# Dense experts: VectorE's instructions in the order of the source, and the source laid out for it

## The chip, the cores and the metric

The kernel runs on one core of one Trainium2 chip. The metric is the device time of one execution in microseconds; lower is better. Three runs of the kernel before gave 3190.89, 3192.01 and 3199.44 us; the median is 3192.01 us.

## The reference

One encoder block on 1024 tokens of width 1024: a mixer (differential attention and a short convolution, gated and summed), then a product-key expert layer (PEER), and a final norm. The change concerns the expert layer. For every token it is

```python
q = (xc @ w_query).reshape(c, 8, 2, 128)
sc = einsum('chpd,hpnd->chpn', q, sub_keys)            # 8 heads, 2 halves, 128 keys
# top 16 of each half, their 256 sums, top 16 of those: 16 of 16384 experts a head
eidx, g = chosen experts, softmax of their scores      # 128 experts a token
a = gelu(einsum('chkd,cd->chk', expert_u[eidx], xc))
out = einsum('chk,chkd->cd', g * a, expert_v[eidx])
```

with `expert_u` and `expert_v` of 16384 x 1024 values, float32. The result is added to h and normed.

## The kernel before

The 1024 tokens are 8 tiles of 128. The expert layer treats them in two ways at once.

*Dense.* For the first five tiles (`NB = 5`, 640 tokens) every expert is computed, 128 experts (one row of the key grid) at a time, in a loop of `NK = 128` rows. For row i `expert_in` (L916) loads u's 128 experts (`raw_rows`), splits them into a rounded high half and a low half (`split`, L893: ScalarE rounds to `uh`, VectorE subtracts to `uhl`), multiplies them with the tokens' two halves into PSUM (`z`: two column halves of 320, 24 matmuls each), applies Gelu on ScalarE (`pr`, L929), multiplies by the router weights `wt` on VectorE (L930; four rows of weights are one load from `w_d`), and splits the product (`ph` on ScalarE, `phl` on VectorE, by the same `split`). `expert_v` (L934) loads and splits the row's v (`vh`, `vhl`). Rows are taken in pairs (`BLK = 2`): `expert_out` (L946) adds a finished pair to the outputs during the two following rows, five of ten output groups in each, six matmuls of 512 columns a group. Four of the ten stay in PSUM (`held`); six go through a PSUM ring of two (`pout`) and are added to SBUF by VectorE (`hacc`, L957). So a row has 48 matmuls of 320 columns and 30 of 512, and on VectorE one `uhl`, `vhl`, `pr` and `phl` and three `hacc`.

*Gathered.* For the last three tiles (`NA = 3`) only the chosen experts are computed. `gather_gen` (L729) goes through 3 x 128 experts. For each, POOL issues an indirect DMA that brings every token's u and v (128 rows of 8 KB) into one of four slots (`uvt`, `UVT = 4`); VectorE takes the dot product with the token (L749), ScalarE applies Gelu and the softmax weight (`wt`, L751 and L752), and VectorE adds the scaled v to the accumulator (`acc`, L754), which also frees the slot. After 128 experts the tile is normed and stored (`last`, L762). The choice itself (`select_gen`, L594: top-16 searches, one-hot sums with a product on POOL, L639, and an exponential on ScalarE) runs for these tiles beside the dense rows, too.

What sets the order: the side jobs are Python generators. Every group of matmuls calls `tick` with its length in source microseconds (at 2.4 GHz, 12.8 us a row, 1638 for the loop), and a generator with a pace of p us makes one step for every p us ticked. The gather has two steps an expert (dot, accumulation) and a pace of `GATHER = 1.9`; a selection has 32 steps a tile, at 1.5 us for tile 5 and `SEL_STEP_D = 8` for tiles 6 and 7. That gives the order of the source. It is then the framework's scheduler that, by priority (order of the source) and readiness in a model of the machine's times, orders each engine's instructions, VectorE's too; on the chip every engine runs its list in that order. After the loop `finish_rows` adds, norms and stores the dense tiles, with the rest of the gather's steps between.

Of the kernel before, what the change touches and what calls it, by code (L numbers as in the profile page):

```python
# [10 lines left out]
F32 = mybir.dt.float32  # L11
# [4 lines left out]
AF = mybir.ActivationFunctionType  # L16
ALU = mybir.AluOpType
# [3 lines left out]
P = 128  # L21
S = 1024
D = 1024
NT = S // P
KD = D // P
NB = 5
NA = NT - NB
# [8 lines left out]
NK = 128  # L36
# [6 lines left out]
NE = PH * TOPK  # L43
# [4 lines left out]
BLK = 2  # L48
NR = 2
WB = 4  # L50
WT = 32
WQ = 4
WFB = 2
GATHER = 1.9
SEL_STEP = 1.5
SEL_STEP_D = 8
W_STEP = 1.6
MIXW = 3
ATT = (5, 4)
# [6 lines left out]
def block_kernel(ctx, tc, x, wqkv, wcols, wpr, wo, wq, skT, uv, uT, an_w, fn_w, fin_w, sub_w,  # L66
                 conv_w, lq1, lk1, lq2, lk2, cosT, sinT, out):
    nc = tc.nc
    V, A, PL, PE, SP = nc.vector, nc.scalar, nc.gpsimd, nc.tensor, nc.sync
# [72 lines left out]
    gens = []  # L142

    def start(gen, us):
        gens.append([gen, us, us])
        return gens[-1]
# [351 lines left out]
    def run(gen):  # L498
        for _ in gen:
            pass  # L500
# [158 lines left out]
    state, got = {}, {}  # L659

    def select_gen_all(t):
        for tt in range(NT):
            while tt not in ready:
                yield
            if tt < NB:
                ev = [state["wfe"].tile([P, NE], F32, name=f"e{j}", tag=f"e{j}", bufs=2) for j in range(3)]
                yield from select_gen(t, tt, ev[:2], ev[2])
                chosen.append(ev)
            else:
                yield from select_a(t, tt)  # L670
                yield SEL_STEP_D

    def select_a(t, tt):
        idx = idxp.tile([P, NE], I32, name="idx", tag="idx")
# [53 lines left out]
    def gather_gen(gat):  # L728
        st = {}  # L729

        def slot():
            return gat.tile([P, 2 * D], F32, name="uvt", tag="uvt", bufs=UVT)

        def fetch(c, k):
            if k == 0:
                st[c] = gat.tile([P, D], F32, name="hng", tag="hng")
                SP.dma_start(out=st[c], in_=hn_d[sels[c][0] * P:(sels[c][0] + 1) * P, :])
            t = slot()
            PL.indirect_dma_start(out=t[:], out_offset=None, in_=uv,  # L739
                                  in_offset=bass.IndirectOffsetOnAxis(ap=sels[c][1][:, k:k + 1], axis=0))  # L740
            return c, k, t

        def use(c, k, t):
            u, v = t[:, 0:D], t[:, D:2 * D]
            if k == 0:
                st["acc"] = gat.tile([P, D], F32, name="acc", tag="acc")
                SP.dma_start(out=st["acc"], in_=h_d[sels[c][0] * P:(sels[c][0] + 1) * P, :])
            zt = tiny.tile([P, 1], F32, name="zt", tag="zt")
            V.scalar_tensor_tensor(u, u, 1.0, st[c], op0=ALU.mult, op1=ALU.mult, accum_out=zt)  # L749
            wt = tiny.tile([P, 1], F32, name="wt", tag="wt")  # L750
            A.activation(wt, zt, AF.Gelu)  # L751
            A.activation(wt, wt, AF.Copy, scale=sels[c][2][:, k:k + 1])  # L752
            yield
            V.scalar_tensor_tensor(st["acc"], v, wt, st["acc"], op0=ALU.mult, op1=ALU.add)  # L754
            yield

        def fetch_last(c):
            t = slot()
            SP.dma_start(out=t[:, 0:D], in_=bass.AP(tensor=fin_w.tensor, offset=fin_w.offset, ap=[[0, P], [1, D]]))
            return t[:, 0:D], t[:, D:2 * D]  # L760

        def last(c, fw, junk):  # L762
            acc = st["acc"]
            ss = tiny.tile([P, 1], F32, name="ss_o", tag="ss_o")
            A.activation(junk, acc, AF.Square, accum_out=ss)
            r = rstd_of(ss, D, 1, "o")
            state["normed"] = c
            yield
            V.scalar_tensor_tensor(acc, acc, r, fw, op0=ALU.mult, op1=ALU.mult)
            SP.dma_start(out=out[sels[c][0] * P:(sels[c][0] + 1) * P, :], in_=acc)  # L770

        held = None
        for c in range(NA):
            while c >= len(sels):
                yield
            for k in range(NE):
                while k >= got[sels[c][0]]:
                    yield
                new = fetch(c, k)
                if held:  # L780
                    end = fetch_last(c - 1) if k == 0 else None
                    yield from use(*held)
                    if end:
                        yield from last(c - 1, *end)
                held = new
        end = fetch_last(NA - 1)
        yield from use(*held)
        yield from last(NA - 1, *end)

    selst, wfs, mts = ExitStack(), ExitStack(), ExitStack()  # L790
    for st in (selst, wfs, mts):
# [94 lines left out]
    ps_v = pspool("ps_v", 2, left)  # L886
    ps_r = pspool("ps_r", 1, left)
    du, dn, dv, hp, gat = (pool(n) for n in ("du", "dn", "dv", "hp", "gat"))
    gather = start(gather_gen(gat), GATHER)
    hacc = hp.tile([P, NB - NR, D], F32, name="hacc")  # L890
    held = [[ps_r.tile([P, 512], F32, name=f"held{t}{hf}") for hf in range(2)] for t in range(NR)]

    def split(t, tag, bufs, shape, eng):  # L893
        pl = du if tag == "uh" else dv
        hi = pl.tile(shape, F32R, name=tag, tag=tag, bufs=bufs)
        A.copy(out=hi, in_=t)  # L896
        lo = pl.tile(shape, F32R, name=f"{tag}l", tag=f"{tag}l", bufs=bufs)
# [13 lines left out]
    def raw_rows(src):  # L911
        t = du.tile([P, D], F32, name="raw", tag="raw", bufs=3)
        SP.dma_start(out=t, in_=src)
        return t

    def expert_in(i):  # L916
        b = i // WB
        if i % WB == 0:
            wts[b] = dn.tile([P, GB // WT, WB, WT], F32, name="wt", tag="wt", bufs=2)
            SP.dma_start(out=wts[b], in_=w_d[:, :, i:i + WB, :].rearrange("c p i t -> p c i t"))  # L920
        ur = raw_rows(uT[i])
        u = split(ur, "uh", 2, [P, D], V)
        us = [(u[0][:, k * P:(k + 1) * P], u[1][:, k * P:(k + 1) * P]) for k in range(KD)]
        hs = halves(GB)
        z = ps_z.tile([P, 2, 512], F32, name="z", tag="z")[:, :len(hs), :hs[0][1]]
        for j, (c0, cn) in enumerate(hs):
            passes(z[:, j, :], us, [(hh[:, k, c0:c0 + cn], hl[:, k, c0:c0 + cn]) for k in range(KD)], cn)
        p = dn.tile([P, GB], F32, name="pr", tag="pr", bufs=1)
        A.activation(p.rearrange("p (h c) -> p h c", h=len(hs)), z, AF.Gelu)  # L929
        V.tensor_mul(p.rearrange("p (c t) -> p c t", t=WT), p.rearrange("p (c t) -> p c t", t=WT),  # L930
                     wts[b][:, :, i % WB, :])
        return split(p, "ph", PHB, [P, GB], V)

    def expert_v(i):  # L934
# [8 lines left out]
            if q:  # L943
                order.append(q.pop(0))

    def expert_out(pv, vv, part, first, last):  # L946
        n = len(order) // BLK
        for t, hf in order[part * n:(part + 1) * n]:
            ds = slice(hf * 512, (hf + 1) * 512)
            lhs = [(p[0][:, t * P:(t + 1) * P], p[1][:, t * P:(t + 1) * P]) for p in pv]  # L950
            rhs = [(v[0][:, ds], v[1][:, ds]) for v in vv]
            if t < NR:
                passes(held[t][hf], lhs, rhs, 512, first, last)
            else:
                ps = ps_v.tile([P, 512], F32, name="pout", tag="v")
                passes(ps, lhs, rhs, 512)
                V.tensor_add(hacc[:, t - NR, ds], ps, hacc[:, t - NR, ds])  # L957
# [20 lines left out]
            SP.dma_start(out=out[t * P:(t + 1) * P, :], in_=ys[t])  # L978
            yield

    pv, vv = [], []
    for i in range(NK + BLK):
        if i < NK:
            pv.append(expert_in(i))
        b, part = i // BLK - 1, i % BLK
        if b >= 0:
            expert_out(pv[:BLK], vv[:BLK], part, b == 0, b == NK // BLK - 1)
            if part == BLK - 1:
                pv, vv = pv[BLK:], vv[BLK:]
        if i < NK:  # L990
            vv.append(expert_v(i))
        if i == 1:
            for t in range(NR, NB):
                SP.dma_start(out=hacc[:, t - NR, :], in_=h_d[t * P:(t + 1) * P, :])
# [9 lines left out]
        next(gather[0])  # L1004
    run(rows)
    run(gather[0])


def _pack(w, kt, cols):
# [50 lines left out]
```

## Time and profile before

| | |
|---|---|
| median of three runs | 3192.01 us |
| profiled execution, its own time | 3202.99 us |
| its span, first to last instruction | 3201.2 us |
| TensorE matmul busy | 3023.5 us, 94% |
| VectorE busy | 2648.8 us, 83% |
| ScalarE, POOL busy | 1300.8 us (41%), 928.5 us (29%) |
| DMA | 801 MB, mean 250 GB/s |

PE is TensorE's matmul, PEld its weight load, DVE VectorE, ACT ScalarE, POOL GpSimd, SP the engine that issues most DMAs. L905 is line 905 of the kernel; helpers (L905 for every dense matmul, L898 for every low half) have one line for all their uses, so groups go by tiles: `phl<-pr,ph` is the subtraction that writes `phl`. Times are microseconds from the start of the span, mean lengths nanoseconds. Matmuls overlap, and their ends are modelled: the pace of matmuls is read from a run of them, not from their lengths. A wait is put down to what was ready last. The dense loop lies between 1317 and 3158 us.

### The profile page before, as it was taken

How to read it: one execution, taken by the hardware profiler on the slowest of the kernel's cores; microseconds unless marked ns; L12 is line 12 of the kernel's file. 1: busy time of each engine (PE TensorE's matmuls, PEld its weight loads, DVE VectorE, ACT ScalarE, POOL GpSimd, SP SyncE). 2: the span in 40 equal slices, each digit the busy share in tenths (PEclk: the TensorE clock that was granted, in tenths of full speed). 3: DMA queues.
4: the chain of work that ended last, by engine and by line, in shares of the span. 5: the costliest groups of instructions: out<-in, count | busy, mean ns of one | idle time of the engine just before them, and what ended most of it. 6: DMA issues, size and time to landing. Idle time of an engine off the chain costs nothing.

```text
span 3201.2 us, 45898 instructions
## 1 busy us (share of the span) xinstructions
PE 3023.5 (94%) x17551; PEld 2773.3 (87%) x17551; DVE 2648.8 (83%) x4661; ACT 1300.8 (41%) x2341; POOL 928.5 (29%) x712
## 2 busy tenths in 40 slices
PE   7999999898989989799999999999999999999994
PEld 6799998798988879789989989899898999999993
DVE  5442466379999996799999999999988999999998
ACT  3322364336567766433333333333333333333332
POOL 2310000036344444222332322222222323332333
PEclk9999999999999989899999999999999999999997
DMA  4451232555444375769888888798888999998987
GB/s 179 145 181 66 83 113 79 199 172 212 145 171 168 135 282 190 255 246 329 311 282 328 316 292 307 278 329 314 302 318 319 345 342 335 341 347 321 340 318 276
DMA packets 237549, 801.11 MB, mean 250 GB/s; under 512 B 18832, under 2 KB 123280, under 8 KB 174096
## 3 DMA queue, kind: packets, MB, share of 16 engines
q0 software_dynamic: 64704, 442.53, 37.3%
q1 hardware_dynamic: 152592, 305.30, 27.6%
q10 hardware_dynamic: 20032, 50.34, 4.1%
q8 instruction: 138, 2.26, 0.3%
q14 instruction: 83, 0.68, 0.1%
HBM read 714.74 MB, written 83.36 MB: 249 GB/s over the span
## 4 chain that ended last, share of the span: by engine, by line
PE 40%; issue 21%; DVE 16%; POOL 9%; DMA 9%; ACT 4%; SPq 0%; POOLq 0%; ACTq 0%; DVEq 0%
PE z L905 9%; POOL uvt L739 8%; PE pout L905 5%; PE pg L228 4%; PE held L905 4%; PE pq L228 3%; DMA uvt<-in_uv,idx 3%; PE ph L228 3%; DVE acc L754 2%; PE py L228 2%; DVE uvt L749 2%; PE pw L695 1%; PE ps L376 1%; PE pv L228 1%; DVE ms L714 1%
## 5 line engine op out<-in xcount | busy, mean ns | idle before, releaser
L739 POOL DMA_INDIRECT uvt<-in_uv,idx x384 | 533.2, 1389 | 1288.1 <-DVE acc L754 937.3
L905 PE MATMUL z<-actTh,uhl 128*128 128x320 f32 x2048 | 638.0, 312 | 4.0 <-DVE uhl L898 4.0
L905 PE MATMUL z<-actTh,uh 128*128 128x320 f32 x2048 | 637.4, 311 | 4.0 <-ACT pr L929 3.0
L905 PE MATMUL z<-actTl,uh 128*128 128x320 f32 x2048 | 637.0, 311 | 0.0
L749 DVE SCALAR_TENSOR_TENSOR uvt<-uvt,hng 128x1024 f32<-128x1024 f32 x384 | 471.4, 1230 | 54.3 <-DMA uvt<-in_uv,idx 53.6
L754 DVE SCALAR_TENSOR_TENSOR acc<-uvt,wt,acc 128x1024 f32<-128x1024 f32 x384 | 495.0, 1289 | 1.6 <-ACT wt L752 1.2
L905 PEld LDWEIGHTS z<-actTh,uh 128*128 128x128 f32 x2048 | 387.7, 189 | 15.7 <-ACT pr L929 3.7
L905 PEld LDWEIGHTS z<-actTh,uhl 128*128 128x128 f32 x2048 | 388.3, 190 | 11.6 <-DVE uhl L898 5.6
L905 PEld LDWEIGHTS z<-actTl,uh 128*128 128x128 f32 x2048 | 387.8, 189 | 9.9
L905 PE MATMUL pout<-vh,ph 128*128 128x512 f32 x768 | 304.0, 396 | 26.9 <-DVE hacc L957 14.0
L905 PE MATMUL pout<-vhl,ph 128*128 128x512 f32 x768 | 302.6, 394 | 0.6 <-DVE vhl L898 0.6
L905 PE MATMUL pout<-vh,phl 128*128 128x512 f32 x768 | 301.8, 393 | 0.0
L957 DVE TENSOR_TENSOR hacc<-pout,hacc 128x512 f32<-128x512 f32 x384 | 260.1, 682 | 21.2 <-PE pout L905 20.5
L718 POOL TENSOR_TENSOR o<-ms,wtr 128x512 f32<-128x512 bf16 x160 | 203.5, 1314 | 254.8 <-PE pw L695 134.8
L185 DVE TENSOR_TENSOR wl<-wr,wh 128x2048 fp32r<-128x2048 f32 x66 | 157.8, 2392 | 113.0 <-ACT wh L184 112.8
L751 ACT ACTIVATE wt<-zt 128x1 f32<-128x1 f32 x384 | 77.0, 201 | 417.0 <-DVE uvt L749 410.8
L896 ACT CAST uh<-raw 128x1024 fp32r<-128x1024 f32 x128 | 134.3, 1049 | 211.3 <-DMA raw<-in_uT 204.5
L184 ACT CAST wh<-wr 128x2048 fp32r<-128x2048 f32 x74 | 141.1, 1908 | 168.0 <-DMA wr<-in_wq 44.7
L695 PE MATMUL pw<-o,o 128*128 128x128 f32 x1280 | 172.3, 288 | 36.9 <-POOL o L718 19.4
L695 PEld LDWEIGHTS pw<-o,o 128*128 128x128 f32 x1280 | 164.4, 202 | 44.7 <-POOL o L718 25.3
L929 ACT ACTIVATE pr<-z 128x640 f32<-128x640 f32 x128 | 90.1, 704 | 275.4 <-PE z L905 254.6
L905 PE MATMUL held<-vhl,ph 128*128 128x512 f32 x512 | 200.3, 392 | 0.1
(290 smaller groups left out, 6758.6 us busy)
## 6 DMA issues: line engine op xcount, KB each, us to landing
raw<-in_uT SPq DMA_DIRECT2D x128, 512.0 KB
raw<-in_uv SPq DMA_DIRECT2D x128, 512.0 KB
w_d<-wbuf ACTq DMA_DIRECT2D x20, 2048.0 KB
wt<-w_d SPq DMA_DIRECT2D x32, 1280.0 KB
wr<-in_wcols SPq DMA_DIRECT2D x28, 1024.0 KB
wr<-in_wq SPq DMA_DIRECT2D x24, 1024.0 KB
xt<-in_x SPq DMA_DIRECT2D x16, 512.0 KB
q_d<-qt POOLq DMA_DIRECT2D x32, 256.0 KB
```

The costliest lines, as they stand in the source:

```text
L184: A.copy(out=op[0][sl], in_=src)
L185: lo.tensor_sub(op[1][sl], src, op[0][sl].bitcast(F32))
L228: PE.matmul(pd, lhsT=l[a], rhs=r[b], start=i == 0 and j == 0, stop=i == n - 1 and j == len(c) - 1)
L695: PE.matmul(pw[:, u, :], lhsT=o2[:, t + u, :], rhs=o1[:, t + u, :], start=True, stop=True)
L718: PL.tensor_tensor(out=o1.rearrange("p t i -> p i t"), in0=ms[:, 0], in1=w[:, ts].unsqueeze(1).broadcast_to(sh), op=ALU.mult)
L739: PL.indirect_dma_start(out=t[:], out_offset=None, in_=uv, in_offset=bass.IndirectOffsetOnAxis(ap=sels[c][1][:, k:k + 1], axis=0))
L749: V.scalar_tensor_tensor(u, u, 1.0, st[c], op0=ALU.mult, op1=ALU.mult, accum_out=zt)
L754: V.scalar_tensor_tensor(st["acc"], v, wt, st["acc"], op0=ALU.mult, op1=ALU.add)
L896: A.copy(out=hi, in_=t)
L905: PE.matmul(ps, lhsT=lhs[k][a], rhs=rhs[k][b], start=first and k == 0 and j == 0, stop=last and k == n - 1 and j == 2)
L929: A.activation(p.rearrange("p (h c) -> p h c", h=len(hs)), z, AF.Gelu)
L957: V.tensor_add(hacc[:, t - NR, ds], ps, hacc[:, t - NR, ds])
```

## The change

In the dense stage, from just before the first row to the end of the kernel, VectorE's instructions are issued in the order of the source (`tc.manual_schedule`); the other engines are scheduled as before. The source is laid out anew:

- `expert_in` is taken apart. `expert_u(i+1)` (load and split of u) stands between the two halves of row i's z; `expert_z` ends with the Gelu; `expert_p` (product with the weights, split) stands behind the first of the row's five output groups.
- In the gather the dot of expert k stands ahead of the accumulation of k-1. A tile's h is loaded with its first gather. The normed tile is written to the second half of the slot that holds the norm's weights, no longer onto `acc`.
- The gather's pace is 2.36 us a step while the selection runs and 1.78 after it; a step of the selection comes every 13 us. The selection of tile 5 is brought to its first 64 experts before the loop.

```diff
-GATHER = 1.9
+GATHER = (2.36, 1.78)
-SEL_STEP_D = 8
+SEL_STEP_D = 13
...
             else:
                 yield from select_a(t, tt)
-                yield SEL_STEP_D
...
         def fetch(c, k):
             if k == 0:
...
+                st["acc", c] = gat.tile([P, D], F32, name="acc", tag="acc")
+                SP.dma_start(out=st["acc", c], in_=h_d[rows, :])
...
-        def use(c, k, t):
...
+        def dot(c, k, t):
+            u = t[:, 0:D]
             zt = tiny.tile([P, 1], F32, name="zt", tag="zt")
             V.scalar_tensor_tensor(u, u, 1.0, st[c], op0=ALU.mult, op1=ALU.mult, accum_out=zt)
             wt = tiny.tile([P, 1], F32, name="wt", tag="wt")
             A.activation(wt, zt, AF.Gelu)
             A.activation(wt, wt, AF.Copy, scale=sels[c][2][:, k:k + 1])
-            yield
-            V.scalar_tensor_tensor(st["acc"], v, wt, st["acc"], op0=ALU.mult, op1=ALU.add)
-            yield
+            return c, k, t, wt, fetch_last() if k == NE - 1 else None
...
+        def accumulate(c, k, t, wt, end):
+            acc = st["acc", c]
+            V.scalar_tensor_tensor(acc, t[:, D:2 * D], wt, acc, op0=ALU.mult, op1=ALU.add)
             yield
+            if end:
+                fw, y = end
+                ss = tiny.tile([P, 1], F32, name="ss_o", tag="ss_o")
+                A.activation(y, acc, AF.Square, accum_out=ss)
+                if c < NA - 1:
+                    yield
+                r = rstd_of(ss, D, 1, "o")
+                state["normed"] = c
+                yield
+                V.scalar_tensor_tensor(y, acc, r, fw, op0=ALU.mult, op1=ALU.mult)
+                SP.dma_start(out=out[sels[c][0] * P:(sels[c][0] + 1) * P, :], in_=y)
...
                 new = fetch(c, k)
                 if held:
+                    held = dot(*held)
+                    yield
+                    if dotted:
+                        yield from accumulate(*dotted)
+                    dotted = held
                 held = new
...
-    gather = start(gather_gen(gat), GATHER)
+    while not sels:
+        next(sel[0])
+    sel[1:] = [SEL_STEP_D, SEL_STEP_D]
+    ordered = ExitStack()
+    ordered.enter_context(tc.manual_schedule(engines={V.engine}))
+    gather = start(gather_gen(gat), GATHER[0])
...
+    def expert_u(i):
+        u = split(raw_rows(uT[i]), "uh", 2, [P, D], V)
+        return [(u[0][:, k * P:(k + 1) * P], u[1][:, k * P:(k + 1) * P]) for k in range(KD)]
+
+    def expert_z(i, us, mid):
...
         for j, (c0, cn) in enumerate(hs):
             passes(z[:, j, :], us, [(hh[:, k, c0:c0 + cn], hl[:, k, c0:c0 + cn]) for k in range(KD)], cn)
+            if j == 0:
+                mid()
         p = dn.tile([P, GB], F32, name="pr", tag="pr", bufs=1)
         A.activation(p.rearrange("p (h c) -> p h c", h=len(hs)), z, AF.Gelu)
+        return p
+
+    def expert_p(i, p):
         V.tensor_mul(p.rearrange("p (c t) -> p c t", t=WT), p.rearrange("p (c t) -> p c t", t=WT),
-                     wts[b][:, :, i % WB, :])
+                     wts[i // WB][:, :, i % WB, :])
         return split(p, "ph", PHB, [P, GB], V)
...
-    def expert_out(pv, vv, part, first, last):
+    def expert_out(pv, vv, part, first, last, after):
         n = len(order) // BLK
-        for t, hf in order[part * n:(part + 1) * n]:
+        for j, (t, hf) in enumerate(order[part * n:(part + 1) * n]):
+            if j == 1:
+                after()
...
-    pv, vv = [], []
+    pv, vv, us = [], [], [expert_u(0)]
     for i in range(NK + BLK):
+        b, part = i // BLK - 1, i % BLK
+        made = []
+        gather[2] = GATHER[sel not in gens]
+
+        def ahead():
+            if i + 1 < NK:
+                us.append(expert_u(i + 1))
+
+        def product():
+            if made:
+                pv.append(expert_p(i, made.pop()))
+
         if i < NK:
-            pv.append(expert_in(i))
...
+            made.append(expert_z(i, us.pop(0), ahead))
         if b >= 0:
-            expert_out(pv[:BLK], vv[:BLK], part, b == 0, b == NK // BLK - 1)
...
+            expert_out(pv[:BLK], vv[:BLK], part, b == 0, b == NK // BLK - 1, product)
+        product()
+        if b >= 0 and part == BLK - 1:
+            pv, vv = pv[BLK:], vv[BLK:]
         if i < NK:
             vv.append(expert_v(i))
```

## Rows read from the trace of the kernel before

**Rows 1.** The page's head: span; each engine's busy us, share, instructions.

```profile
span 3201.2 us, 45898 instructions
...
PE 3023.5 (94%) x17551; PEld 2773.3 (87%) x17551; DVE 2648.8 (83%) x4661; ACT 1300.8 (41%) x2341; POOL 928.5 (29%) x712
```

**Rows 2.** Busy time of each engine by stretch; the first line names the columns.

```profile
core 0: us, PE busy (x) PEld busy (x) DVE busy (x) ACT busy (x) POOL busy (x), PEclk, DMA share, GB/s
1346.00:1450.00 104.00, 98.85 (x531) 89.56 (x532) 100.11 (x207) 33.05 (x66) 27.44 (x18) 0.95 0.75 260
1450.00:2600.00 1150.00, 1135.90 (x6295) 1029.87 (x6295) 1091.74 (x1697) 392.51 (x801) 334.88 (x242) 1.00 0.87 313
2600.00:3147.00 547.00, 545.90 (x3040) 497.11 (x3039) 510.65 (x647) 189.41 (x403) 176.35 (x124) 1.00 0.91 334
3147.00:3201.20 54.20, 8.57 (x28) 5.24 (x26) 40.04 (x50) 12.26 (x34) 17.25 (x11) 0.61 0.69 247
sum 1855.20, PE 1789.22 PEld 1621.78 DVE 1742.55 ACT 627.23 POOL 555.92; mean PE 447.31 PEld 405.44 DVE 435.64 ACT 156.81 POOL 138.98
```

**Rows 3.** Pieces of the chain, 2100 to 2200 us: start us, us, what.

```profile
2144.42 4.10 PE held L905 x18
...
2151.57 5.04 PE z L905 x34
```

**Rows 4.** TensorE's waits from 1346 us on: us, times, longest.

```profile
PE pout L905 <- DVE hacc L957: 14.0, 10, 4.8
PE pout L905 <- ACT ph L896: 12.9, 1, 12.9
```

**Rows 5.** VectorE's waits from 1346 us on, same columns.

```profile
DVE uvt L749 <- DMA uvt<-in_uv,idx: 53.6, 48, 2.7
DVE hacc L957 <- PE pout L905: 20.5, 30, 1.9
DVE uhl L898 <- ACT uh L896: 15.1, 5, 7.6
DVE pr L930 <- ACT pr L929: 12.3, 14, 2.1
DVE pr L930 <- DMA wt<-w_d: 8.4, 1, 8.4
...
DVE phl L898 <- ACT ph L896: 0.2, 1, 0.2
```

**Rows 6.** Timeline of the end: start us, us, engine line op, what, count.

```profile
3157.77 0.40 PE L905 MATMUL pout<-vh,phl 128*128 128x512 f32 x1
...
3197.48 0.33 SPq L770 DMA_DIRECT2D out<-acc  x1
```

**Rows 7.** Timeline, VectorE and ScalarE at the first product.

```profile
1346.36 0.82 DVE L930 TENSOR_TENSOR pr<-pr,wt 128x640 f32<-128x640 f32 x1 [8.37 <-DMA wt<-w_d]
...
1347.10 0.08 DVE L590 MATCH_VALUE_LOAD tk<-sv,sc 128x8 f32 x1
...
1347.27 0.72 ACT L896 CAST ph<-pr 128x640 fp32r<-128x640 f32 x1 [11.14 <-DVE pr L930]
...
1348.09 0.80 DVE L898 TENSOR_TENSOR phl<-pr,ph 128x640 fp32r<-128x640 f32 x1
```

**Rows 8.** Timeline, a selection's product on POOL and phl beside it.

```profile
1409.76 2.85 POOL L639 TENSOR_TENSOR sc<-sc,sf 128x1024 bf16<-128x1024 bf16 x1 [0.48 <-DVE sc L637]
...
1410.73 2.57 DVE L898 TENSOR_TENSOR phl<-pr,ph 128x640 fp32r<-128x640 f32 x1
```

**Rows 9.** Pieces of the chain that are a gather, issue to use.

```profile
1421.49 11.22 DMA uvt<-in_uv,idx
...
1915.49 7.12 DMA uvt<-in_uv,idx
```

**Rows 10.** VectorE after 3147 us, groups: count, busy us, mean ns, idle.

```profile
L754 DVE SCALAR_TENSOR_TENSOR acc<-uvt,wt,acc 128x1024 f32<-128x1024 f32 x12 | 15.4, 1280 | 1.4 <-ACT wt L752 1.2
L749 DVE SCALAR_TENSOR_TENSOR uvt<-uvt,hng 128x1024 f32<-128x1024 f32 x10 | 12.2, 1220 | 7.1 <-DMA uvt<-in_uv,idx 7.0
```

More of the change, by code (lines that the diff above doesn't have):

```diff
@@ L736, in fetch @@
                 st[c] = gat.tile([P, D], F32, name="hng", tag="hng")
-                SP.dma_start(out=st[c], in_=hn_d[sels[c][0] * P:(sels[c][0] + 1) * P, :])
+                rows = slice(sels[c][0] * P, (sels[c][0] + 1) * P)
+                SP.dma_start(out=st[c], in_=hn_d[rows, :])
+                st["acc", c] = gat.tile([P, D], F32, name="acc", tag="acc")
+                SP.dma_start(out=st["acc", c], in_=h_d[rows, :])
             t = slot()
@@ L741, in fetch @@
             return c, k, t
-        def use(c, k, t):
[L744 to L747, printed above, removed]
+        def dot(c, k, t):
+            u = t[:, 0:D]
             zt = tiny.tile([P, 1], F32, name="zt", tag="zt")
@@ L752, in use, with fetch_last @@
             A.activation(wt, wt, AF.Copy, scale=sels[c][2][:, k:k + 1])
-            yield
-            V.scalar_tensor_tensor(st["acc"], v, wt, st["acc"], op0=ALU.mult, op1=ALU.add)
-            yield
-        def fetch_last(c):
+            return c, k, t, wt, fetch_last() if k == NE - 1 else None
+        def fetch_last():
             t = slot()
@@ L760, in fetch_last @@
             return t[:, 0:D], t[:, D:2 * D]
[L762 to L767, printed above, removed]
-            yield
-            V.scalar_tensor_tensor(acc, acc, r, fw, op0=ALU.mult, op1=ALU.mult)
-            SP.dma_start(out=out[sels[c][0] * P:(sels[c][0] + 1) * P, :], in_=acc)
-        held = None
+        def accumulate(c, k, t, wt, end):
+            acc = st["acc", c]
+            V.scalar_tensor_tensor(acc, t[:, D:2 * D], wt, acc, op0=ALU.mult, op1=ALU.add)
+            yield
+            if end:
[9 more added lines that the diff above has]
+                SP.dma_start(out=out[sels[c][0] * P:(sels[c][0] + 1) * P, :], in_=y)
+        held = dotted = None
         for c in range(NA):
@@ L780, in gather_gen @@
                 if held:
[L781 to L784, printed above, removed]
+                    held = dot(*held)
[3 more added lines that the diff above has]
+                    dotted = held
                 held = new
-        end = fetch_last(NA - 1)
-        yield from use(*held)
-        yield from last(NA - 1, *end)
+        held = dot(*held)
+        yield
+        yield from accumulate(*dotted)
+        yield from accumulate(*held)
     selst, wfs, mts = ExitStack(), ExitStack(), ExitStack()
@@ L914, in raw_rows @@
         return t
-    def expert_in(i):
+    def expert_u(i):
+        u = split(raw_rows(uT[i]), "uh", 2, [P, D], V)
+        return [(u[0][:, k * P:(k + 1) * P], u[1][:, k * P:(k + 1) * P]) for k in range(KD)]
+    def expert_z(i, us, mid):
         b = i // WB
@@ L920, in expert_in @@
             SP.dma_start(out=wts[b], in_=w_d[:, :, i:i + WB, :].rearrange("c p i t -> p c i t"))
-        ur = raw_rows(uT[i])
-        u = split(ur, "uh", 2, [P, D], V)
-        us = [(u[0][:, k * P:(k + 1) * P], u[1][:, k * P:(k + 1) * P]) for k in range(KD)]
         hs = halves(GB)
@@ L979, in finish_rows @@
             yield
-    pv, vv = [], []
+    pv, vv, us = [], [], [expert_u(0)]
     for i in range(NK + BLK):
+        b, part = i // BLK - 1, i % BLK
[7 more added lines that the diff above has]
+                pv.append(expert_p(i, made.pop()))
         if i < NK:
-            pv.append(expert_in(i))
-        b, part = i // BLK - 1, i % BLK
+            made.append(expert_z(i, us.pop(0), ahead))
         if b >= 0:
-            expert_out(pv[:BLK], vv[:BLK], part, b == 0, b == NK // BLK - 1)
-            if part == BLK - 1:
-                pv, vv = pv[BLK:], vv[BLK:]
+            expert_out(pv[:BLK], vv[:BLK], part, b == 0, b == NK // BLK - 1, product)
+        product()
+        if b >= 0 and part == BLK - 1:
+            pv, vv = pv[BLK:], vv[BLK:]
         if i < NK:
@@ L1006, in block_kernel @@
     run(gather[0])
+    ordered.close()
 def _pack(w, kt, cols):
```

## Prediction, before the changed kernel was run

> **What bounds the kernel now.** I read the page's head first. TensorE's matmuls are busy for 94% of the span and VectorE for 83%, ScalarE for 41% and POOL for 29% [rows 1]; so I asked how these two share the dense-expert stage. The table by stretches is the second view [rows 2]: from 1346 us, where the first router weights arrive, to 3147 us VectorE is busy for 100.1 + 1091.7 + 510.7 = 1702.5 of 1801 us, then for 40.0 of the last 54.2. The dense loop has 128 rows, so a row takes 1801/128 = 14.07 us.
>
> Is TensorE full in those rows? The third view is pieces of the chain in which it runs without a break [rows 3]: 5.04/34, so 0.148 us for a matmul of 320 columns, and 4.10/18, so 0.228 us for one of 512. A row has 2 x 24 of the first (z) and 5 x 6 of the second (five output groups, three passes for each row of the pair): 48 x 0.148 + 30 x 0.228 = 13.94 us. That is 0.13 us less than the measured row: TensorE is the bound, and its own waits in the stage are small (14.0 us on hacc, 12.9 us once at the start [rows 4]).
>
> VectorE is close behind. Its busy time from 1346 us on is 1742.5 us, 13.6 us a row. Its idle time is 1855.2 - 1742.5 = 112.7 us: 53.6 waiting for gathered experts, 20.5 for pout, 15.1 for uh, 12.3 + 8.4 for pr [rows 5], the rest at the end. The last stretch is the tail: TensorE's last matmul starts at 3157.77 us, and the last store is issued at 3197.48 us [rows 6]; in between VectorE ends the gathered experts that were left over.
>
> The Trainium skill (Perfetto Trace Analysis, "Identifying the Most-Contended Engine") says to judge TensorE's headroom not by matmul time but by the busy share of weight loads. That is 497.1/547 = 91% here and would leave 9%, some 160 us of the 1801; the cadence of rows 3 leaves 1%, and I go by the cadence.
>
> **The change part by part.** The arithmetic stays: the same dots, accumulations, subtractions and selections, so VectorE's 1742.5 us stay. What changes is the order, and in it what VectorE waits for.
>
> *Waits that go.* With VectorE late, pout is ready when hacc comes to it, and pr is made (the product stands behind the first output group): of 20.5 + 12.3 us I keep 5. The low half of u is made a row ahead, so of 15.1 us I keep 5, for late loads. Together 10 us (between 0 and 48).
>
> *A wait that comes: phl.* `expert_p` issues three things in a row: VectorE's product pr, ScalarE's rounding of it to ph, VectorE's subtraction phl. There is no step of a generator between them. Before, the scheduler put other work between product and subtraction, so phl waited only 0.2 us in all 128 rows. In the order of the source nothing can stand there. The price can be read at 1346 us [rows 7]: pr starts at 1346.36 and the next instruction on VectorE at 1347.10, so pr costs 0.74; ScalarE rounds from 1347.27 to 1347.99; phl starts at 1348.09, behind another instruction. Alone it could start between 1347.99 and 1348.09; I take 1348.03. VectorE would stand still from 1347.10 to there: 0.93 us. Times 128 rows: 119 us. From below 0.85 x 128 = 109, if the hand-overs are quicker; from above 135, since ScalarE is busy for 34% of the time [rows 2] and the rounding can come behind a cast: 34% of half of 0.72 us, 0.12 us a row more. Behind the waiting subtraction all of VectorE's queue stands: the gather's accumulations, and so POOL's next gathers, and hacc, and so TensorE's next output group. Nothing covers it: a row of VectorE's is 13.6 + 0.93 = 14.5 us, over TensorE's 13.94.
>
> *Selection in order.* Five half selections lie in the ordered stretch. Each waits twice for POOL's product (L639) and once for ScalarE's exponential. A POOL product lasts 2.85 us in the row shown, but in that same time phl takes 2.57 us [rows 8] where 0.80 is usual [rows 7]; so before, most of that time was lost as well. I take 10 x 1.1 + 5 x 1.0 = 16 us; bounds are 0 and 10 x 2.85 + 5 x 1.0 = 33. The Trainium skill (SBUF — State Buffer, "Who interferes with whom") has it that a VectorE instruction with two SBUF inputs and a GpSimd one that reads SBUF shut each other out; the two rows agree. By that rule the 11 us for POOL would be near 0, without it near 28.
>
> *The gather.* An expert's slot (there are four) is freed by its accumulation. Before, dot and accumulation alternate, and from the accumulation of expert k-4 to the dot of k there are 7 steps of 1.9 us of source pace; by the real row (14.07 for 12.8 us of pace) 14.6 us. Now the dot goes ahead, and there are 5 steps: 11.8 and 8.9 us of pace, and with rows of 14.9 us (12.8 of pace) 13.7 us in the first phase and 10.4 in the second. A gather takes 7.12 to 11.22 us from issue to use where it was waited for [rows 9]. So the first phase is covered and the second is at the edge. I take 30 us instead of 53.6: below 0, above 0.8 us (11.2 less 10.4) for each of some 168 experts of the second phase, 134 us. The phases: 80 steps of selection at 13 us make 1040 of 1638 us of pace, hence 1040/2.36 = 441 and 598/1.78 = 336 steps, 777 for 768 that are needed, so the gather ends with the loop.
>
> *The tail and the rest.* The tail's work is in the 1742.5 us already; its idle 14.2 us I keep (5 to 20). That the normalized rows go to another tile than acc frees acc before its store has landed; the next tile's acc now waits for its load twice. I set these against each other. The start is held by the weights at 1346 us as before.
>
> **Sum.** 1346 + 1742.5 + 119 + 16 + 30 + 10 + 14 = 3277.5 us of span. The profiled execution took 1.8 us more than its span and is 0.34% above the median, so 3279.3 x 0.9966 = 3268 us, 2.4% above 3192. All low ends together (1346 + 1742.5 + 109 + 5) give 3193 at the median, all high ends 3449. Neither is likely, and the ends aren't independent, since a longer row gives the gathers more time: its own range is 3210 to 3335.
>
> **Rivals.**
> *Faster, TensorE stays the bound.* TensorE could give back its 14.0 us on hacc, and if the gather ends with it, the experts that VectorE now does after 3147 us, 15.4 + 12.2 us [rows 10], leave the tail: 3201.2 - 14.0 - 27.6 = 3159.6 of span, 3150 at the median. VectorE has room for 3159.6 - 1346 - 1742.5 - 14 = 57 us of waits then. For it: TensorE is the bound now, and 112.7 us of idle VectorE show that the scheduler's order leaves something. Against it: phl alone has 119. Even to break with before, at 98.7 us of waits ahead of the tail, phl may have 98.7 - 56 = 43, 0.33 us a row; from there on it is this case, and rows 7 show nearly three times that. (By the weight-load rule of the skill, TensorE could give back more, and VectorE's busy time would be the floor: 1346 + 1742.5 + 14, 3094 at the median.)
> *No change.* The waits that come and those that go cancel: VectorE's idle time stays at 113 us, which needs phl at its low end and nothing else. 3192.
> *Slower still, the gather starves.* In the second phase a row asks for 3.6 gathers of 1.05 MB, two of 0.52 MB and 0.33 MB of weights, 5.2 MB in 14.9 us, 347 GB/s. The stretch to 3147 ran at 334 GB/s with the DMA engines 91% busy, 367 at 100% [rows 2]. If the gathers stretch to their longest, the second phase pays 134 instead of 30 us: 3372. Against it: a late gather also slows the asking.
>
> **Chances.** Forecast 0.62, starving gather 0.08, no change 0.10, TensorE-bound 0.20. About 0.3% is what a measurement of this kernel can tell from no change, so faster 0.20, same 0.10, slower 0.70. The range runs from 3150 to 3335: it leaves out the lower half of the faster case and the starving one.
>
> **What would show it.** Right: 100 to 135 us of VectorE idle before phl, put down to ScalarE's ph, some 0.9 us in nearly all 128 rows; hacc's wait for pout near 0, and instead TensorE waiting for hacc for 100 us or more; rows of 14.6 to 15 us; the last matmul within 25 us of the end. Wrong in size: waits for gathers well off 30 us, to be looked for in the second phase. Wrong altogether: phl without a wait, or rows under 14.0 us.

## The result, and the profile after

The changed kernel takes 3374.35 us (median of 4 runs, 3368.91 to 3384.74) against 3191.96 for the one before on the same chip: a ratio of 1.057, with a 95% interval of 1.054 to 1.060. It is slower, as forecast, but by 5.7% where 2.4% was forecast. The time lies above the range.

The page's head and the table by stretches (columns as in [rows 2]) answer to [rows 1, 2]:

```profile
span 3370.7 us, 45675 instructions
...
PE 3086.2 (92%) x17551; PEld 2769.9 (82%) x17551; DVE 2655.0 (79%) x4661; ACT 1299.9 (39%) x2341; POOL 885.9 (26%) x712
```

```profile
1346.00:1450.00 104.00, 103.19 (x578) 93.43 (x577) 89.91 (x157) 33.37 (x65) 23.32 (x18) 1.00 0.80 279
1450.00:2600.00 1150.00, 1070.50 (x5760) 942.79 (x5759) 1002.91 (x1633) 355.17 (x710) 275.80 (x211) 0.99 0.78 275
2600.00:3330.00 730.00, 668.15 (x3526) 574.99 (x3524) 634.93 (x804) 228.41 (x505) 208.30 (x161) 0.99 0.87 316
3330.00:3370.70 40.70, 14.63 (x54) 11.32 (x54) 29.80 (x38) 10.51 (x23) 3.95 (x4) 0.74 0.52 199
sum 2024.70, PE 1856.47 PEld 1622.53 DVE 1757.55 ACT 627.46 POOL 511.36; mean PE 464.12 PEld 405.63 DVE 439.39 ACT 156.87 POOL 127.84
```

From 1346 us on VectorE is busy for 1757.55 us, 15.0 more than before, and idle for 2024.7 - 1757.55 = 267.1 us, where it was 112.7 and where the forecast had 119 + 16 + 30 + 10 + 14 = 189. So the forecast span of 3277.5 is missed by 93.2 us: 15.0 of work and 78.2 of waits. Over the whole span VectorE does as much as before (2655.0 us against 2648.8), in a longer time.

The waits of VectorE from 1346 us on (us in all, times, longest) answer to [rows 5], and those of TensorE to [rows 4]:

```profile
DVE phl L908 <- ACT ph L906: 165.2, 121, 6.1
DVE uvt L748 <- DMA uvt<-in_uv,idx: 30.4, 33, 2.7
DVE e L640 <- POOL sc L639: 20.7, 10, 2.1
DVE hacc L975 <- PE pout L915: 13.7, 22, 1.9
DVE zz L647 <- ACT tv L645: 6.5, 5, 2.0
DVE acc L761 <- DMA acc<-h_d: 4.8, 2, 2.6
DVE phl L908 <- issue: 4.8, 6, 0.8
```

```profile
PE pout L915 <- DVE hacc L975: 62.8, 52, 7.1
PE z L915 <- DVE uhl L908: 60.2, 53, 4.5
PE z L915 <- ACT pr L942: 15.5, 19, 2.7
```

The wait at phl is there, as forecast; it is 165.2 + 4.8 us, not 119 (the page's group of all 128 has 170.7). TensorE, which before waited 14.0 us for hacc, now waits for VectorE at two places, 123 us in all. Its last matmul ends at 3350.9 us, so a row takes (3350.9 - 1346)/128 = 15.66 us.

Why is phl's wait so long? Where nothing disturbs it, the timeline of VectorE shows what [rows 7] let one expect:

```profile
1409.50 0.83 DVE L946 TENSOR_TENSOR pr<-pr,wt 128x640 f32<-128x640 f32 x1
1411.12 0.82 DVE L908 TENSOR_TENSOR phl<-pr,ph 128x640 fp32r<-128x640 f32 x1 [0.79 <-ACT ph L906]
```

From start to start 1.62 us, less the 0.74 that pr costs when work follows it: 0.88 us a row, against 0.93 forecast. But 0.79 is only the usual gap (81 of the 128 are 0.79 or 0.80 us, none is shorter); 38 are over 1.2 and 22 over 2 us. The longest, as the chain of work that ended last has it (start us, us, what):

```profile
1934.47 1.23 DVE vhl L908
1935.70 0.02 issue
1935.72 11.68 DMA raw<-in_uT
1947.40 0.02 issue
1947.42 1.04 ACT uh L906
1948.46 0.64 ACT ph L906
1949.10 0.02 issue
1949.12 0.82 DVE phl L908
```

Here pr had started on VectorE at 1942.19. ScalarE would have rounded it within a microsecond, but the next instruction in ScalarE's queue was the cast of a later row's u, whose rows landed only at 1947.40; ph came behind it. That load had been issued the moment vhl freed its slot, one of three. So the chain goes in a ring: VectorE frees a slot, the load takes 11.68 us, ScalarE's queue stands still for it, and VectorE's queue stands still for ScalarE. It is the same in 36 of the 38 long waits: shortly ahead of ph ScalarE runs a cast of u that has waited for its load. The Trainium skill ("PSUM — Partial Sum Buffer", section "Engine vs sequencer instructions") says that the queues of ScalarE, VectorE and GpSimd are strictly first in, first out; these rows agree.

### The profile page after: what moved, and what is told of

It is laid out like the page before. It is cut to its first block, busy times and chain, and to the rows that moved or that the text cites. A ratio compares the mean times of both kernels' runs of the same rounds, so it can differ in the third digit from the quotient of the medians.

```text
span 3370.7 us, 45675 instructions
## 1 busy us (share of the span) xinstructions
PE 3086.2 (92%) x17551; PEld 2769.9 (82%) x17551; DVE 2655.0 (79%) x4661; ACT 1299.9 (39%) x2341; POOL 885.9 (26%) x712
## 4 chain that ended last, share of the span: by engine, by line
PE 28%; issue 23%; DVE 23%; DMA 10%; POOL 9%; ACT 6%; SPq 0%; POOLq 0%; ACTq 0%; DVEq 0%
POOL uvt L741 7%; DMA raw<-in_uT 5%; PE pg L228 5%; DVE acc L761 4%; PE z L915 3%; DVE uvt L748 3%; PE pq L228 3%; PE ph L228 2%; DVE hacc L975 2%; DVE vhl L908 2%; PE pw L694 2%; PE py L228 2%; DMA uvt<-in_uv,idx 1%; PE pout L915 1%; PE ps L376 1%
## 5 line engine op out<-in xcount | busy, mean ns | idle before, releaser
L741 POOL DMA_INDIRECT uvt<-in_uv,idx x384 | 493.1, 1284 | 1487.7 <-DVE acc L761 1436.8
L915 PE MATMUL z<-actTh,uhl 128*128 128x320 f32 x2048 | 646.8, 316 | 74.3 <-DVE uhl L908 74.2
L748 DVE SCALAR_TENSOR_TENSOR uvt<-uvt,hng 128x1024 f32<-128x1024 f32 x384 | 467.4, 1217 | 57.7 <-DMA uvt<-in_uv,idx 30.4
L915 PE MATMUL pout<-vh,ph 128*128 128x512 f32 x768 | 315.4, 413 | 64.2 <-DVE hacc L975 62.8
L975 DVE TENSOR_TENSOR hacc<-pout,hacc 128x512 f32<-128x512 f32 x384 | 262.0, 685 | 13.9 <-PE pout L915 13.7
L915 PEld LDWEIGHTS pout<-vh,ph 128*128 128x128 f32 x768 | 147.6, 192 | 118.3 <-DVE hacc L975 92.4
L908 DVE TENSOR_TENSOR phl<-pr,ph 128x640 fp32r<-128x640 f32 x128 | 105.7, 826 | 170.7 <-ACT ph L906 166.0
```

What stands on the lines that cost most here:

```text
L741: PL.indirect_dma_start(out=t[:], out_offset=None, in_=uv, in_offset=bass.IndirectOffsetOnAxis(ap=sels[c][1][:, k:k + 1], axis=0))
L915: PE.matmul(ps, lhsT=lhs[k][a], rhs=rhs[k][b], start=first and k == 0 and j == 0, stop=last and k == n - 1 and j == 2)
```

## The experiments

The two theories at the outset. A: VectorE's queue in the order of the source is the cost; each wait in it is paid, the one at phl above all. B: the new layout (dot ahead, other paces, other tiles) costs as much, or what is taken from one wait comes back at the next. Each expectation below names its own theories by letters. One point of the ratio is 32 us; the change stands at 1.057.

| run | what | median us | ratio to before, 95% interval |
|---|---|---|---|
| e2 | layout without the order | 3200.58 | 1.0009, 0.9994 to 1.0024 |
| e7 | old layout, in order | 4079.76 | 1.2750, 1.2726 to 1.2775 |
| e3 | a second rounding in phl's round trip | 3440.75 | 1.0758, 1.0735 to 1.0781 |
| e1 | phl behind the second output group | 3330.74 | 1.0413, 1.0386 to 1.0441 |
| e4 | a fourth raw buffer | 3333.86 | 1.0439, 1.0410 to 1.0468 |
| e5 | e1 and e4 | 3311.51 | 1.0352, 1.0331 to 1.0372 |
| e9 | ScalarE in order too | 3538.91 | 1.1069, 1.1047 to 1.1090 |
| e6 | vhl on GpSimd, in order | 3421.01 | 1.0687, 1.0664 to 1.0710 |
| e8 | vhl on GpSimd, kernel before | 3290.63 | 1.0283, 1.0262 to 1.0304 |
| e11 | hng from GpSimd's queue | 3379.36 | 1.0579, 1.0559 to 1.0600 |
| e12 | e5, e11 and steps in the selection | 3277.85 | 1.0259, 1.0238 to 1.0279 |
| e10 | e2 with a fourth raw buffer | 3201.39 | 1.0017, 1.0005 to 1.0030 |
| e13 | before, faster gather | 3198.27 | 1.0013, 1.0000 to 1.0026 |
| e14 | e10, faster gather | 3201.87 | 1.0013, 1.0000 to 1.0027 |

**Order or layout: e2 and e7.** e2 takes out the order alone:

```
     ordered = ExitStack()
-    ordered.enter_context(tc.manual_schedule(engines={V.engine}))
     gather = start(gather_gen(gat), GATHER[0])
```

> The changed layout (u a row ahead, dot ahead of accumulation, paces 2.36 and 1.78, selection every 13 us) with VectorE's order given back to the scheduler. Theory A (the order costs, not the layout): phl's wait under 5 us, waits in selection under 5 us, the time within 1% of 3192 us. Rival B (the layout costs: shorter lead of the gathers, faster second phase): uvt's wait over 80 us and the time over 3280 us.

It is level with the kernel before, and phl waits for nothing in it. The layout by itself costs nothing; the 5.7% come with the order. e7 is the reverse, the kernel before with those lines put in:

> The kernel before, its old layout and old paces, with VectorE alone in the order of the source. Theory A (the new layout shortens waits that the old one would have in order: u's low half right behind its cast, the product right behind the gelu of the same row, the accumulation right behind its dot): slower than the change, 3450 to 3800 us, with waits at uhl and pr of several us in each row. Rival B (the layout does little, the order is the whole cost): 3340 to 3410 us.

It takes 4080 us, more than either expected, and its waits are where the layout takes them away:

```profile
DVE pr L932 <- ACT pr L931: 523.9, 122, 11.6
DVE acc L754 <- ACT wt L752: 200.9, 165, 4.3
DVE phl L900 <- ACT ph L898: 100.4, 127, 0.8
```

In the same order, then, the layout saves some 700 us; what it leaves is phl. TensorE waits longer in e7 and is granted a lower clock there, on average 0.90 of 2.4 GHz against 0.97 in the change; how much of the 700 us that is no run tells. Note that here phl has only its usual gap in every row.

**Is phl's wait on the path: e3, e1.** e3 doubles the round trip:

```
+        A.copy(out=p, in_=p)
         return split(p, "ph", PHB, [P, GB], V)
```

> ScalarE copies pr onto itself once more ahead of the rounding, so the round trip from the product to phl is one ScalarE instruction of about 0.7 us longer in each of the 128 rows (the values stay the same). Theory A: phl's wait grows by 128 x 0.65 to 0.75, so 83 to 96 us, and the time by as much, to 3457 to 3470 us. Rival B (the wait at phl lies in slack): phl's wait grows and others shrink, and the time stays within 25 us of 3374.

From 1346 us on:

```profile
DVE phl L908 <- ACT ph L906: 258.2, 127, 5.2
```

The wait at phl rises by 88 us, from 170.0. The time rises by 1.9 points, 60 us, and the profiled span by 67: two thirds to three quarters of the wait are paid. e1 takes the subtraction out of the product and puts it one output group later (`after[0]` issues pr and ph, `after[1]` phl):

```
             if j == 1:
-                after()
+                after[0]()
+            if j == 2:
+                after[1]()
```

> The product with the router weights and its rounding stay behind the first output group; the subtraction that writes phl moves behind the second, so that a pass's gather steps and mostly one hacc stand between. Theory A (VectorE is the bound and stands still at phl: 171 us in the changed kernel, 99 of it as 128 times the bare round trip of 0.77 us, 72 as ScalarE's lateness): the 99 go and about half of the 72, phl's wait falls to some 35 us, and the time from 3374 to about 3240 us. Rival B (VectorE's place in the row is set by something else, such as the gather's shorter lead or TensorE): phl's wait goes, but reappears at uvt or hacc, and the time stays over 3330 us.

1.6 points, some 50 us, come off, far less than A had; at 3330.74 us the time is B's by less than a microsecond, though phl's wait did not fall as far as either had it. The waits of e1 tell why:

```profile
DVE phl L957 <- ACT ph L949: 92.8, 63, 9.3
DVE uvt L748 <- DMA uvt<-in_uv,idx: 51.2, 39, 3.5
DVE hacc L987 <- PE pout L915: 27.9, 36, 2.6
```

Half of the rows have no wait at phl left; the others still have long ones, up to 9.3 us. Other work on VectorE covers the round trip, but not a cast that waits for a load. And some of what is won comes back: gathers and pout are now waited for 20.8 and 14.2 us longer.

**The late cast: e4, e9, e5.** e4 gives the loads a fourth slot, so that one is issued earlier:

```
-        t = du.tile([P, D], F32, name="raw", tag="raw", bufs=3)
+        t = du.tile([P, D], F32, name="raw", tag="raw", bufs=4)
```

> Four buffers instead of three for the loads of u and v, nothing else. Theory C (the 38 waits at phl that are longer than 1.2 us are ScalarE's cast of a later row's u, which stands ahead of ph in ScalarE's queue and waits for its load): loads start about half a row sooner, the long waits go, phl's wait falls from 171 towards 105 us, TensorE's wait for uhl from 74 to under 40, and the time to about 3310 us. Rival D (the long waits come from full DMA engines, so that a load that starts sooner lands no sooner): phl's wait stays over 150 us and the time within 20 us of 3374.

The long waits are gone: 125 of 128 are 0.8 us or less, and from 1346 us on the wait is 104.5 us.

```profile
DVE phl L908 <- ACT ph L906: 104.5, 127, 3.8
...
DVE hacc L975 <- PE pout L915: 21.6, 25, 2.8
...
DVE vhl L908 <- ACT vh L906: 11.0, 24, 0.8
```

So the wait has two parts, about 104 us of round trip and 66 of late casts, and the fourth slot takes the second; the span falls by 39.9, and 7.9 more is waited for pout and 10.7 more at vhl. So C's cause is right, but its time, about 3310 us, was not reached, and TensorE's wait for uhl fell from 74.2 to 50.7 us (from 1340 us on), not under 40. e9 tests the same from the other side, with no more buffers. In the source the cast of the later u stands behind p's; only ScalarE's order, which the scheduler works out, put it ahead.

```
-    ordered.enter_context(tc.manual_schedule(engines={V.engine}))
+    ordered.enter_context(tc.manual_schedule(engines={V.engine, A.engine}))
```

> The change with ScalarE in the order of the source as well, where the cast of u two rows ahead stands behind the cast of p, not ahead of it. Theory A (the long waits at p's low half come from that cast alone, put ahead by an order worked out with earlier landings): all 128 waits at p's low half go to about 0.8 us, some 100 us in sum against 171, and the time to 3320 to 3345 us, as with a fourth raw buffer. Rival B (the late load of u is what costs, and it shows at u's own low half or at TensorE instead): 3360 to 3385 us. Rival C (ScalarE in order has waits of its own, the expert's weight behind a gelu that waits for TensorE): over 3400 us.

```profile
DVE uhl L908 <- ACT uh L906: 108.3, 95, 2.2
DVE phl L908 <- ACT ph L906: 97.5, 123, 0.8
DVE hacc L975 <- PE pout L915: 77.3, 51, 3.9
```

On the mechanism A holds: no wait at phl is over 0.8 us. On the time C does: 3539 us. The late cast now delays u's own low half, and TensorE waits 223.9 us for ScalarE's gelu, up to 23.2 at once. An order in a second queue costs more than the one misplaced cast. e5 takes both parts of the wait, with the edits of e1 and e4:

```
-        t = du.tile([P, D], F32, name="raw", tag="raw", bufs=3)
+        t = du.tile([P, D], F32, name="raw", tag="raw", bufs=4)
...
+            if j == 2:
+                after[1]()
```

> The change with both: p's low half taken behind the second output group, and a fourth buffer for the raw rows. Theory A (two separate costs at the same instruction: the round trip over ScalarE, and a later u's cast that stands ahead of p's in ScalarE's queue until its load lands): the first kernel lost the second cost on its 63 remaining waits, the second one the first cost on all 128 rows, so together the wait at p's low half falls under 15 us and the time to 3374 - 40 - 44 - 20 to 40 = 3250 to 3270 us. Rival B (what is taken from this wait is given back at the next one, since a row's length is set elsewhere): not under 3310 us.

```profile
DVE uvt L748 <- DMA uvt<-in_uv,idx: 53.2, 40, 3.5
DVE hacc L987 <- PE pout L915: 49.5, 45, 5.7
DVE phl L957 <- ACT ph L949: 28.8, 48, 3.2
...
DVE vhl L908 <- ACT vh L906: 12.7, 27, 1.4
```

The result is B's, by little: of the 141 us that phl's wait lost, the span kept 62. The waits for gathers, pout and vh took up 22.8 + 35.8 + 12.4 = 71. This is half-way between the theories: the wait at phl is paid, but with it gone VectorE stands more before the next operands in its fixed order.

**Less work on VectorE: e6, e8.**

```
-        return split(vr, "vh", VHB, [P, D], V)
+        return split(vr, "vh", VHB, [P, D], PL)
```

> The change with v's low half (127 subtractions of 128x1024, 1.2 us each, some 150 us) on GpSimd instead of VectorE. Theory A (VectorE's queue, work and waits one behind the other, sets the length of a row): most of the 150 us comes off, 3230 to 3280 us. Rival B (a row's length is set by the round of TensorE, ScalarE and VectorE through z and p, and VectorE's own amount of work hardly matters): within 40 us of 3374. Rival C (GpSimd's subtraction slows VectorE's own instructions or the gather's issue): no gain, and VectorE's means go up by over 5%.

> The kernel before (no order) with v's low half on GpSimd: 150 us of VectorE's 1742 us behind 1346 us gone. Theory A (before, TensorE and VectorE stand close to each other, TensorE's matmuls alone need down to about 3150 us): 3150 to 3185 us. Rival B (TensorE is the bound already, or the gather): 3186 to 3200 us. Rival C (GpSimd's work slows VectorE or the gather's issue): over 3200 us.

Both came out as C. In e6 VectorE's dots, accumulations and halves of u became slower by 15 to 37%, and so they did in e8, whose groups (count, busy us, mean ns) show the price:

```profile
L754 DVE SCALAR_TENSOR_TENSOR acc<-uvt,wt,acc 128x1024 f32<-128x1024 f32 x384 | 589.4, 1535 | 19.7 <-ACT wt L752 18.1 <-DVE acc L754 0.5
L749 DVE SCALAR_TENSOR_TENSOR uvt<-uvt,hng 128x1024 f32<-128x1024 f32 x384 | 574.4, 1497 | 19.5 <-DMA uvt<-in_uv,idx 11.4 <-DMA hng<-hn_d 8.0
L957 DVE TENSOR_TENSOR hacc<-pout,hacc 128x512 f32<-128x512 f32 x384 | 261.4, 683 | 10.7 <-PE pout L905 10.6
L898 DVE TENSOR_TENSOR uhl<-raw,uh 128x1024 fp32r<-128x1024 f32 x124 | 192.4, 1552 | 8.2 <-ACT uh L896 7.4 <-issue 0.7
```

149 us of vhl left VectorE, but acc, dot and uhl, which took 495.0, 471.4 and 152.5 us before, took 94.4 + 103.0 + 39.9 = 237 more. The 90 us by which the span grew are about the difference.

**Start and selection: e11, e12.** The +15.0 us of work: before, VectorE had done 12.4 us of halves and selection between 1317 and 1346 us, now 7.1, which is 5.3 of it. Its queue stands at the first dot:

```profile
1338.12 1.22 DVE L748 SCALAR_TENSOR_TENSOR uvt<-uvt,hng 128x1024 f32<-128x1024 f32 x1 [25.49 <-DMA hng<-hn_d]
```

e11 loads hng from another queue:

```
-                SP.dma_start(out=st[c], in_=hn_d[rows, :])
+                (PL if c == 0 else SP).dma_start(out=st[c], in_=hn_d[rows, :])
```

> The change with the first tile's normalized rows (hng) loaded from GpSimd's queue instead of SyncE's, where the load stood behind the load of the weights wt and the first dot waited 25.5 us for it. Theory A (VectorE's whole queue stood still in this wait, and some 15 us of halves and dots that before were done by then moved behind it): the wait falls under 10 us, the time by 8 to 18 us to 3356 to 3366. Rival B (the first row waits for wt in any case until about 1341 us, so nothing is won): 3369 to 3380 us.

Nothing is won, but not for B's reason. The same dot waits as long, now for the gathered rows themselves:

```profile
1334.28 1.22 DVE L748 SCALAR_TENSOR_TENSOR uvt<-uvt,hng 128x1024 f32<-128x1024 f32 x1 [24.47 <-DMA uvt<-in_uv,idx]
```

The first gather starts only at 1322 us in this run and at 1325 in the change, and is used 12 and 13 us later: two landings end there at about the same time, and the wait goes to whichever is the later. e12 adds to e5 the edit of e11 and a step of other work in the selection:

```
-SEL_STEP_D = 13
+SEL_STEP_D = 11
...
                 PL.tensor_tensor(out=oh, in0=oh, in1=sfv[:, :, j, :].unsqueeze(3).broadcast_to(sh), op=ALU.mult)
+                if tt >= NB:
+                    yield
                 V.tensor_reduce(out=ev[j][:, a * 64:(a + 1) * 64].rearrange("p (h k) -> p h k", k=TOPK),
...
             A.activation(tv, dv, AF.Exp)
+            if tt >= NB:
+                yield
```

> The change with p's low half behind the second output group, a fourth raw buffer, hng from GpSimd's queue, and a step of other work between the selection's product on GpSimd and its sum on VectorE, and between its exponential and its sum (step pace 11 instead of 13). Theory A (each of these waits stands on VectorE's queue, so what they cost adds): 3311 less about 12 for the start and 20 to 28 for the selection, 3268 to 3282 us. Rival B (what is taken from one wait comes back at the next): 3295 to 3312 us.

3277.85 us: A. The selection's waits (20.7 and 8.0 us in e5) are gone from the list, which now reads

```profile
DVE uvt L752 <- DMA uvt<-in_uv,idx: 52.4, 43, 3.8
DVE hacc L991 <- PE pout L919: 26.4, 32, 2.0
DVE phl L961 <- ACT ph L953: 24.7, 47, 0.8
DVE vhl L912 <- ACT vh L910: 13.8, 26, 2.0
DVE uvt L752 <- DMA hng<-hn_d: 12.3, 2, 7.0
```

The wait for pout is lower by 23.1 us than in e5, too, and that for hng higher, 12.3 against 4.9; which of the edits did what was not run apart. More than half of the loss is won back, and the order still costs 2.6%.

**Looking for a version that beats both: e10, e13, e14.** e10 is e2 with e4's fourth slot; e13 and e14 take the faster rival at its word and let the gather run ahead, so that the experts behind the last matmul leave the tail.

```
-GATHER = 1.9
+GATHER = 1.8
...
-GATHER = (2.36, 1.78)
+GATHER = (2.2, 1.7)
```

> The change's layout and paces without the order, and with a fourth raw buffer. Without it VectorE waited 28.6 us for u's cast, and 33 us of ScalarE's waits were for u's load. Theory A (VectorE is what limits this version too, so its waits count): 3175 to 3193 us. Rival B (TensorE and the gather limit it as much): 3194 to 3206 us, no different from the version with three.

> The kernel before with a source pace of 1.8 us instead of 1.9 for the gather, so that its steps end with the loop. Theory A (the rival that forecast faster was right on one point: about 9 experts are accumulated behind the last matmul, some 25 us with their dots, and they can leave the tail while TensorE stays the bound): 3168 to 3188 us. Rival B (VectorE has no room in the rows either: 13.6 us of work and 0.4 to 0.5 us of waits against TensorE's 13.94, so what leaves the tail lengthens the rows): 3190 to 3205 us.

> The change's layout without the order, a fourth raw buffer, and gather paces of 2.2 and 1.7 instead of 2.36 and 1.78 us, for the same question in the new layout, where the dots stand a step ahead. Theory A: 3170 to 3190 us. Rival B: 3193 to 3210 us.

All three are within 0.3% of the kernel before. In e13 as many experts as before, 9, are accumulated behind the last matmul, and VectorE waits longer for gathers:

```profile
DVE uvt L749 <- DMA uvt<-in_uv,idx: 63.8, 46, 6.4
```

In e14 it is 8, against 7 in e10. At these paces a quicker source did not bring the experts out of the tail. No version here beats the kernel before.

## Why the prediction was right in kind and wrong in size

*What bounded the kernel before* is borne out, not shown: without the order neither another layout, nor another slot, nor another pace changes the time (e2, e10, e13, e14), and adding to VectorE's work lengthens it (e8). That fits TensorE with 1% of room and VectorE with 3%; no run took work from TensorE.

*That phl's wait comes and is paid* holds: e2 has no wait and no loss, e3 pays two thirds to three quarters of a longer one. That it alone decides does not: with 141 us of it gone (e5), 3.5% of the 5.7% stay. The account of 0.93 us for the round trip was close (0.88).

*The step that failed* is the upper bound of that wait: "from above 135, since ScalarE is busy for 34% of the time [rows 2] and the rounding can come behind a cast: 34% of half of 0.72 us, 0.12 us a row more". It took ScalarE for an engine that is either busy or free. A queue has a third state: at its head an instruction that waits. ph came behind casts of u that waited for their loads, up to 8.3 us each, and that is 66 of the 170.0 us, as e4 and e9 show from two sides. The row that warned of it is not in the argument, though it stands in the trace of before, among ScalarE's waits from 1346 us on:

```profile
ACT uh L896 <- DMA raw<-in_uT: 202.6, 81, 11.4
```

It was harmless there, since VectorE had other work to do meanwhile. In the change it is

```profile
ACT uh L906 <- DMA raw<-in_uT: 444.4, 121, 8.3
```

because VectorE, being late, also frees the slots late: the queue that issues these loads waits 1173.3 us for vhl, 431.8 before. In e2, with the same layout and no order, ScalarE's wait is 33.3 us; e4 brings it to 59.3.

This step is not the whole miss. With phl at 170.0 us and all else as forecast the sum would give 3319 us, inside the range; the smaller terms carried the time out of it, first among them VectorE's work, which was taken as unchanged without an allowance.

The 93.2 us of span, term by term, from 1346 us on (in time the miss is 106 us; the other 13 are the step from span to time, read from the profiled execution of before):

| term | forecast | measured | miss |
|---|---|---|---|
| phl | 119 | 170.0 | +51.0 |
| VectorE's work from 1346 us on | 1742.5 | 1757.55 | +15.0 |
| selection (20.7 + 6.5) | 16 | 27.2 | +11.2 |
| gathered experts | 30 | 30.4 | +0.4 |
| hacc, pr, uhl (13.7 + 0.9 + 0) | 10 | 14.6 | +4.6 |
| all other idle time, tail among it | 14 | 24.9 | +10.9 |

*The work.* VectorE's total rose by 6.2 us (2655.0 - 2648.8), and 8.8 us more moved behind 1346. "The start is held by the weights at 1346 us as before" did not come so: the first product starts at 1341.55 us and waits for no load. What held VectorE was its first dot, up to 1338.12, and in order it can't use that time for other work. e11 brought 3.6 us of work back ahead of 1346 (10.7 against 7.1) and gained no time, so that it can be had is not shown.

*Selection.* The wait for GpSimd's product was 2.07 us each; 1.1 had been taken because phl beside it took 2.57 us in [rows 8]. In order nothing stands beside it, and the product, 1.93 us on average, is waited for whole. ScalarE's exponential, put at 1.0 us without a row, was waited for 1.3 us each.

*The gather* came out at 30.4 as forecast. So the rival whose time was nearest, 3372 us by gathers that starve, hit the number with the wrong cause.

*The faster rival* fell on the point named: it needed phl's wait under 0.33 us a row, and it is 0.79 at its least. In e13 and e14 a quicker pace didn't get its 27.6 us in the tail either.

*The other signs.* The last matmul ends 19.8 us before the end, within the 25 named. TensorE's wait for hacc was to be 100 us or more; it is 62.8, and the 60.2 at uhl were not named. The rows, at 15.66 us, are over the 14.6 to 15 that would have shown the forecast right.

What stays open: why in e5 the waits for gathers and pout take up 71 us of 141, that is, which of them come from TensorE's own limit and which from the order. e12 shows that the rest can be lowered, not how far.

## What to carry to other kernels

When a queue is put in a fixed order, go through every instruction in it that waits for another engine, and read what that engine's own queue waits for just ahead of the answer: a cast with a late load there costs its landing, not its duration. A round trip between two engines needs other work placed inside it, and the loads that the partner's queue waits for need a buffer more; only both together took most of the wait away, and even then about half of it came back at the next operand. Where two engines are within a few per cent of the bound, an order that the scheduler works out, which fills each wait with other work, was worth 180 us here.

## What the runs showed of the hardware

GpSimd's subtraction of two SBUF tiles slowed only some of VectorE's instructions. In e8 dot, acc and uhl, which read 128x1024 from two SBUF tiles, went from 1230, 1289 and 1229 ns to 1497, 1535 and 1552 on average; hacc, one of whose inputs is in PSUM, stayed at 683 (682 before). In e6 it is the same: dot 1425, acc 1464 and uhl 1676 ns, hacc 685. The timeline of e8 tells which of them met a subtraction of vhl: acc that overlap one took 3.10 us on average (51 of them), the others 1.28 (319); dot 3.36 and 1.23, uhl 2.66 and 1.23, but hacc 0.68 in both cases. pr, also with two SBUF tiles, met none and phl five (828 to 938 ns on average), so they changed less. The Trainium skill ("SBUF — State Buffer", section "Who interferes with whom") says that a VectorE instruction with two SBUF inputs contends with a GpSimd one that reads SBUF, and that one with at most one SBUF input, outside the two-port modes, does not; the two runs agree on both halves. Moving a half to GpSimd was therefore dearer here than leaving it on VectorE: 237 us came for 149 that went.

A load of 512 KB took 11.68 us from issue to landing in the chain shown above, in a stretch where the DMA engines are busy for 78%; with three slots a cast two rows ahead was not far enough ahead for it, and with four (e4) it mostly was.
